# A hybrid decoder step: S5 constants on VectorE, power tables on GpSimd, q and k norms by head pairs, and the S5 state with chunks innermost

## The chip, the core and the metric

The kernel runs on one core of a Trainium2 chip (trn2). Five engines work at once: TensorE (PE in the profile; its weight loads are PEld), VectorE (DVE), ScalarE (ACT), GpSimd (POOL) and SyncE (SP, which here issues DMAs). Each takes its instructions strictly in the order in which the program issues them, and waits for semaphores of the others. The metric is the device time of one execution in microseconds (us).

## The reference

288 token columns (256 of a prompt, and 8 sequences of 4 sampled tokens) pass two layers of width 2048; everything is f32.

```python
# layer 0, first mixer
h = rmsnorm(x, w);  q, k, v, f, u = split(h @ w_in)          # 8 heads of 128; u is 1024 wide
q = rmsnorm(q, q_gain);  k = rmsnorm(k, k_gain)               # over the 128 of each head
logf = log_sigmoid(f + b_f)
att = softmax(q k^T * 128**-0.5 + cumsum(logf) differences, causal) v   # prompt; samples with a paged cache
# S5: 64 groups, 16 inputs and 64 complex states each, a diagonal recurrence over time
a = exp((lam_re + i*lam_im) * exp(log_dt));  z = (a - 1) / lam
s_t = a * s_(t-1) + (z*b) u_t;   y = Re(c s) + d*u;   ssm = gelu(y) * sigmoid(gelu(y) @ w_glu + b_glu)
x += concat(att, ssm) @ w_out
x += swiglu(rmsnorm(x))                                       # 5632 wide; layer 1: causal pooling mixer, then swiglu
```

The outputs also hold k, v, logf and the last S5 states.

## The kernel before, in words

**Weights and units.** Each f32 weight block of [128 x 512] arrives by a DMA of SP (`Ring.load`, L138), ScalarE rounds it to `wh` (L148), VectorE makes the rest `wl` = raw - wh (L149), and TensorE runs three products for each 128 x 128 piece (L186 to L188), whose right side has 288 columns. A *unit* is one such block: 12 matrix instructions. Three units are split ahead (`ring0.look`), in four buffers, so a VectorE that falls behind starves TensorE after three units.

**Ticks set the order.** After each unit `tick()` (L101) runs every pending evacuation, and then one step of each generator in `side`. A generator does some work, yields, and goes on one tick later; `W` holds how many ticks it lets pass. So all side work stands at a place in each engine's queue that this count fixes, whether or not its inputs are ready there. Units in order: 32 for u (ticks 1 to 32), one long one for f (33), 64 for q and k (34 to 97, a head in eight), 32 for v (98 to 129), 16 for the GLU, then w_out. When TensorE's side products are not ready, the units behind them wait too.

**First norm** (`gen_n0`, L372). With n0a = 3 the squares of x go into `acc` at ticks 4 to 11 (ScalarE squares, VectorE adds), and at tick 12 TensorE sums `accs` over partitions (L290). The rstd that comes of it is needed by the evacuations of u's first two blocks (`early`), and the fourth block can't begin before them.

**S5 constants** (`exp32`, `gen_s5_prep`, L417 to L537). Some 100 operations on [128 x 32] and [128 x 64] tiles make dt, |a|, sine and cosine, a's powers 1 to 4 and z: all on GpSimd, but for the reciprocal (L492), which VectorE runs at a fixed place. Then `steps`, `cross` and `times` make the tables a4x and a16x (a to the 4th and 16th), and VectorE forms bb = z*b.

**Power tables** (`powers`, L549). gt holds a^j * bb for j = 0 to 3 and p0 holds c * a^j for j = 0 to 4, real and imaginary part: 24 operations of up to [128 x 480] for gt and 24 of [128 x 512] for p0, all on VectorE, two of three followed by a yield. `gen_s5_g` turns gt by TensorE into gq (L648), and the products bb x p0 (L609) give the kernel of a block of four tokens (`kall`, `mt`).

**S5 over time** (`gen_s5_main`, L707). Time is cut into 64 chunks of four tokens. u goes through DRAM into `ut` (16 DMAs, half of them from GpSimd's queue). xt [73 chunks, 4, 2, 8] takes gq x ut (L750). Then `step` (L731, L735) joins four chunks at a time, three quarters on GpSimd and the last on VectorE; a chain of 15 steps on GpSimd runs over the blocks of four; `fill` (L779 to L785) carries it back into the chunks, one quarter on GpSimd and then three on VectorE. Their `tms` and `car` tiles have two buffers each that both engines share in program order. At last p0 x xt (L808) gives y. In each of these small products two of the array's four 64 x 64 quarters alternate.

**q and k norms** (`gen_qk`, L909), per head: square on ScalarE, split into `sh` and `sl` (VectorE, L917), four one-pass products with a matrix of ones (L922, L923), rsqrt on a tile that holds the sum on all 128 partitions, and two scalings.

Of the kernel before, what the change touches and what calls it, by code (L numbers as in the profile page):

```python
# [7 lines left out]
F32 = mybir.dt.float32  # L8
# [8 lines left out]
W = dict(n0a=3, n0b=0, n0c=0, n0d=2, rec=9, s5a=3, gq=0, xw=0, qk0=2, qk1=2, qk2=0, qk3=1, qk4=0, f=2, m=4, lag=2,  # L17
# [68 lines left out]
def hybrid_step(ctx, tc, I, O):  # L86
# [283 lines left out]
    n0 = Norm(x0, P_MIX0, pool0, "qs", bufs=2)  # L370

    def gen_n0():  # L372
# [8 lines left out]
        G.dma_start(bcd[:, 0], I["s5b"])  # L381
        G.dma_start(bcd[:, 1], I["s5c"])
# [27 lines left out]
    def gstt(out, a, c, b, op0, op1):  # L410

        t = small("stt", (128, 2, 2, 32), "tms", 2)[:, 0]
        t = t if len(out.shape) == 3 else t[:, 0]
        G.tensor_scalar(t, a, c, None, op0=op0)  # L414
        G.tensor_tensor(out, t, b, op1)

    def exp32(out, x):  # L417

        n, r, p = small("am"), small("den"), small("zt")
        e = pool0.tile([128, 32], I32, name="ei", tag="zu")  # L420
        G.tensor_scalar(n, x, 88.0, -87.0, op0=OP.min, op1=OP.max)
        G.tensor_scalar(r, n, 1.4426950408889634, MAGIC, op0=OP.mult, op1=OP.add)
        G.tensor_scalar(r, r, -MAGIC, None, op0=OP.add)
        gstt(p, r, -0.693359375, n, op0=OP.mult, op1=OP.add)
        G.tensor_scalar(e, r, 127.0, 8388608.0, op0=OP.add, op1=OP.mult)
        gstt(r, r, 2.12194440054690583e-4, p, op0=OP.mult, op1=OP.add)
        G.tensor_scalar(p, r, 1.0 / 5040.0, None, op0=OP.mult)
        for c in (1.0 / 720.0, 1.0 / 120.0, 1.0 / 24.0, 1.0 / 6.0, 0.5, 1.0):
            gstt(p, p, c, r, op0=OP.add, op1=OP.mult)
        gstt(out, p, 1.0, e.bitcast(F32), op0=OP.add, op1=OP.mult)  # L430

    def gen_s5_prep():
        lre, lim, ldt = (par[:, o:o + 32] for o in (P_LRE, P_LIM, P_LDT))
        dt, th, mag = small("dt"), small("th"), small("mag")
        exp32(dt, ldt)
        yield
        mul(mag, lre, dt, G)
        exp32(mag, mag)
        mul(th, lim, dt, G)
        yield  # L440
# [4 lines left out]
        for q in range(2):  # L445
            G.tensor_scalar(n[:, q], th, 1.0 / (2.0 * math.pi), 0.25 * q, op0=OP.mult, op1=OP.add)
        G.tensor_scalar(n, n, MAGIC, None, op0=OP.add)
        G.tensor_scalar(n, n, -MAGIC, None, op0=OP.add)
        thb = th[:, None, :].to_broadcast([128, 2, 32])
        gstt(r, n, -C1, thb, op0=OP.mult, op1=OP.add)  # L450
        gstt(r, n, -C2, r, op0=OP.mult, op1=OP.add)
        gstt(r, n, -C3, r, op0=OP.mult, op1=OP.add)
        G.tensor_scalar(r[:, 1], r[:, 1], math.pi / 2.0, None, op0=OP.add)
        yield
        mul(r2, r, r, G)
        fac = [math.factorial(k) for k in range(20)]
        G.tensor_scalar(sc, r2, 1.0 / fac[17], None, op0=OP.mult)
        for k in (15, 13, 11, 9, 7, 5, 3):
            gstt(sc, sc, (-1.0) ** (k // 2) / fac[k], r2, op0=OP.add, op1=OP.mult)
        gstt(sc, sc, 1.0, r, op0=OP.add, op1=OP.mult)  # L460
# [5 lines left out]
        mul(ap[:, 1, 0, :], mag, sc[:, 1], G)  # L466
        mul(ap[:, 1, 1, :], mag, sc[:, 0], G)

        def cross(dst, a):
            G.tensor_copy(dst[:, 0, 0, :], a[:, 0, :])  # L470
            G.tensor_scalar(dst[:, 0, 1, :], a[:, 1, :], -1.0, None, op0=OP.mult)
            G.tensor_copy(dst[:, 1, 0, :], a[:, 1, :])
            G.tensor_copy(dst[:, 1, 1, :], a[:, 0, :])

        cross(a1x, ap[:, 1])
        def times(out, a, bx):
            tm = small("tm", (128, 2, 2, 32), "tms", 2)
            mul(tm, a[:, None].to_broadcast([128, 2, 2, 32]), bx, G)
            add(out, tm[:, :, 0, :], tm[:, :, 1, :], G)

        for j in range(2, 5):
            times(ap[:, j], ap[:, j - 1], a1x)
        yield
        ar, ai = ap[:, 1, 0, :], ap[:, 1, 1, :]
        am, den, t, u = small("am"), small("den"), small("zt"), small("zu")
        zr, zi = small("zr"), small("zi")
        mul(den, lre, lre, G)
        mul(t, lim, lim, G)
        add(den, den, t, G)
        G.tensor_scalar(am, ar, -1.0, None, op0=OP.add)  # L490
        yield from ticks(W["rec"])
        V.reciprocal(den, den)  # L492
        yield
        mul(t, am, lre, G)
        mul(u, ai, lim, G)
        add(t, t, u, G)
        mul(zr, t, den, G)
        mul(t, ai, lre, G)
        mul(u, am, lim, G)
        G.tensor_tensor(t, t, u, OP.subtract)  # L500
        mul(zi, t, den, G)
# [11 lines left out]
        s5["a4"] = steps("a4x", ap[:, 4])  # L513
        a8 = small("a8", (128, 2, 32), "n")
        cross(a1x, ap[:, 4])
        times(a8, ap[:, 4], a1x)
        cross(a1x, a8)
        times(a8, a8, a1x)
        s5["a16"] = steps("a16x", a8)
        yield from ticks(W["s5a"])  # L520
# [21 lines left out]
        count = [0]  # L542

        def pace():
            count[0] += 1
            if count[0] % 3 != 1:
                yield

        def powers(dst, src, j0, pr, neg):  # L549

            nj = 4 if j0 else 3
# [1152 lines left out]
```

## Time and profile before

| | us |
|---|---|
| median of three runs | 2225.29 (2223.77 to 2228.7) |
| the profiled execution, its own time | 2224.44 |
| its span in the trace | 2222.6 |
| TensorE busy in the span | 2186.7 |
| mean granted TensorE clock | 0.995 |

Microseconds in the views count from the start of the span. An idle time in brackets behind a row names what released the instruction. "L149" is line 149 of the kernel before.

### The profile page before, as it was taken

What the parts mean: (1) busy time and instruction counts of PE and PEld (TensorE: products, weight loads), DVE (VectorE), ACT (ScalarE), POOL (GpSimd) and SP (SyncE); (2) the same over time, 40 slices, a digit from 0 to 9 for tenths busy, and PEclk for the clock granted to TensorE, in tenths of its full rate; (3) what the DMA queues carried; (4) which work ended last, traced back from release to release, by engine and by line L of the source; (5) the groups of instructions that cost most, each with busy time, mean ns of one, the idle gap of its engine ahead of it and who ended that gap; (6) DMA issues with size and microseconds to landing.
All of it is one profiled execution on the core that took longest, in us unless ns stands there. A gap on an engine that the chain in (4) does not pass through costs nothing.

```text
span 2222.6 us, 41005 instructions
## 1 busy us (share of the span) xinstructions
PE 2186.7 (98%) x17006; PEld 2146.2 (97%) x17006; DVE 1222.1 (55%) x1595; ACT 918.8 (41%) x1302; POOL 191.4 (9%) x297
## 2 busy tenths in 40 slices
PE   8998999999999999999999999999999999999999
PEld 7987988999999999999999998999999999999999
DVE  6987656655554545444554557555554455455443
ACT  5454545444333333333433355443333333333332
POOL 8365200100000000000000020000000000000000
PEclk9999999999999999999999999999999999999999
DMA  6637487555555555555555653555555555555554
GB/s 202 172 106 199 134 252 251 189 190 171 165 163 167 161 171 162 170 161 172 161 171 158 199 161 106 168 162 169 167 158 170 170 163 162 170 167 165 161 169 141
DMA packets 136715, 376.43 MB, mean 169 GB/s; under 512 B 22352, under 2 KB 26144, under 8 KB 136240
## 3 DMA queue, kind: packets, MB, share of 16 engines
q1 hardware_dynamic: 123008, 358.07, 53.9%
q10 hardware_dynamic: 11728, 11.27, 1.6%
q0 software_dynamic: 1792, 4.47, 0.7%
q8 instruction: 133, 2.18, 0.4%
q14 instruction: 54, 0.44, 0.1%
HBM read 364.34 MB, written 8.76 MB: 168 GB/s over the span
## 4 chain that ended last, share of the span: by engine, by line
PE 89%; POOL 3%; DVE 3%; DMA 2%; issue 1%; ACT 1%; SPq 0%; ACTq 0%; DVEq 0%; POOLq 0%
PE m L186 28%; PE m L188 28%; PE m L187 28%; DVE wl L149 1%; PE s L808 1%; POOL xt L735 1%; DMA pg<-in_vc_dram 1%; POOL stt L414 1%; DMA zs<-zscr 0%; POOL tms L731 0%; ACT wh L148 0%; DMA raw<-in_w_dram 0%; DMA raw<-in_wv_dram 0%; PE s L750 0%; DMA bl<-in_band_dram 0%
## 5 line engine op out<-in xcount | busy, mean ns | idle before, releaser
L149 DVE TENSOR_TENSOR wl<-raw,wh 128x1024 fp32r<-128x1024 f32 (+2 forms) x769 | 819.0, 1070 | 805.1 <-ACT wh L148 801.0
L148 ACT CAST wh<-raw 128x1024 fp32r<-128x1024 f32 (+2 forms) x769 | 692.4, 905 | 942.7 <-PE m L187 756.4
L188 PE MATMUL m<-xh,wl 128*128 128x288 f32 (+1 forms) x3312 | 979.6, 296 | 9.9 <-DVE wl L149 9.9
L186 PE MATMUL m<-xh,wh 128*128 128x288 f32 (+1 forms) x3312 | 987.4, 298 | 0.9 <-DVE x L221 0.9
L187 PE MATMUL m<-xl,wh 128*128 128x288 f32 (+1 forms) x3312 | 978.3, 295 | 0.0
L188 PEld LDWEIGHTS m<-xh,wl 128*128 128x128 f32 (+1 forms) x3312 | 622.5, 188 | 12.7 <-DVE wl L149 12.0
L186 PEld LDWEIGHTS m<-xh,wh 128*128 128x128 f32 (+1 forms) x3312 | 623.2, 188 | 8.6 <-issue 4.8
L187 PEld LDWEIGHTS m<-xl,wh 128*128 128x128 f32 (+1 forms) x3312 | 621.8, 188 | 0.9
L188 PE MATMUL m<-gh,wl 128*128 128x288 f32 x1408 | 415.7, 295 | 0.0
L187 PE MATMUL m<-gl,wh 128*128 128x288 f32 x1408 | 415.3, 295 | 0.0
L186 PE MATMUL m<-gh,wh 128*128 128x288 f32 x1408 | 414.7, 295 | 0.0
L186 PEld LDWEIGHTS m<-gh,wh 128*128 128x128 f32 x1408 | 264.5, 188 | 0.0
L188 PEld LDWEIGHTS m<-gh,wl 128*128 128x128 f32 x1408 | 264.4, 188 | 0.0
L187 PEld LDWEIGHTS m<-gl,wh 128*128 128x128 f32 x1408 | 264.2, 188 | 0.0
L215 ACT ACTIVATE s<-t 128x288 f32<-128x288 f32 x88 | 39.1, 444 | 169.9 <-DVE t L218 169.9
L1380 POOL DMA_DIRECT2D out_plo_dram<-es x1 | 0.6, 575 | 780.2 <-DVE wl L149 780.2
L218 DVE TENSOR_TENSOR t<-m,rstd 128x576 f32<-128x576 f32 x88 | 66.1, 751 | 0.0
L218 DVE TENSOR_TENSOR t<-s,t 128x288 f32<-128x288 f32 x88 | 40.3, 458 | 46.3 <-ACT s L215 46.3
L1336 DVE TENSOR_TENSOR gl<-t,gh 128x288 fp32r<-128x288 f32 x88 | 40.3, 458 | 44.0 <-ACT gh L1335 44.0
L221 DVE TENSOR_TENSOR x<-m,x 128x576 f32<-128x576 f32 x72 | 54.1, 751 | 8.8 <-PE m L188 8.7
L1335 ACT CAST gh<-t 128x288 fp32r<-128x288 f32 x88 | 38.1, 433 | 46.2 <-DVE t L218 46.2
L186 PE MATMUL m<-ssmh,wh 128*128 128x288 f32 x128 | 38.9, 304 | 0.8 <-ACT wh L148 0.8
(349 smaller groups left out, 1426.2 us busy)
## 6 DMA issues: line engine op xcount, KB each, us to landing
raw<-in_w_dram SPq DMA_DIRECT2D x472, 512.0 KB, 3.7
raw<-in_w_dram SPq DMA_DIRECT2D x64, 384.0 KB, 3.2
raw<-in_wqk_dram SPq DMA_DIRECT2D x64, 256.0 KB, 3.2
raw<-in_wout_dram SPq DMA_DIRECT2D x64, 256.0 KB, 3.2
raw<-in_wu_dram SPq DMA_DIRECT2D x32, 256.0 KB, 3.7
pg<-in_kc_dram SPq DMA_DIRECT2D x32, 256.0 KB, 3.4
raw<-in_wv_dram SPq DMA_DIRECT2D x32, 256.0 KB, 3.6
pg<-in_vc_dram SPq DMA_DIRECT2D x28, 256.0 KB, 4.1
```

The lines of the kernel that those rows point to most:

```text
L148: S.copy(h[:, :n], t[:, :n])
L149: self.share().tensor_tensor(l[:, :n], t[:, :n], h[:, :n], OP.subtract)
L186: T.matmul(o, h[:, w0:w0 + m], xh, start=st, stop=False)
L187: T.matmul(o, h[:, w0:w0 + m], xl, start=False, stop=False)
L188: T.matmul(o, l[:, w0:w0 + m], xh, start=False, stop=sp)
L215: S.activation(out, x, func, **kw)
L218: eng.tensor_tensor(out, a, b, OP.mult)
L221: eng.tensor_tensor(out, a, b, OP.add)
L414: G.tensor_scalar(t, a, c, None, op0=op0)
L735: eng.tensor_tensor(dst, dst, tv[:, :, :, c], OP.add)
L1335: S.copy(gs[c][0][:, i, :], t[:, 1, :])
L1336: V.tensor_sub(gs[c][1][:, i, :], t[:, 1, :], gs[c][0][:, i, :])
```

## The change

Everything lies in the first mixer, and the diff below is cut to its new side.

- The S5 constants run on VectorE: 72 operations, with a fused scalar-tensor-tensor in place of each pair on GpSimd, a few at each tick. Seven are issued ahead of the first unit, nine at tick 1, the last at tick 19.
- The first norm starts at tick 9 (n0a = 8), so TensorE's sum stands at tick 17 and `early` is over at tick 24.
- b and c are loaded by SP in the seventh unit, not by GpSimd.
- Of gt the imaginary half goes to GpSimd (12 operations), which then makes a4x and a16x; the real half stays on VectorE. All 24 operations of p0 go to GpSimd, issued at ticks 36 to 39, and bb x p0 stands at ticks 42, 43, 46 and 47.
- All 16 loads of `ut` are issued by ScalarE's queue.
- xt is [4, 16, 73] with the chunk innermost, so the right sides of L808 are contiguous; h0 goes through a `tms` tile.
- L609, L750 and L808 go round all four quarters of the array, into two PSUM banks.
- The q and k norms take two heads at a time: four f32 sums of 32 rows each into the four row groups of one bank, one rsqrt on [128 x 288], and per head two products of 32 rows that spread a row group's result over 128 partitions. The scaling then reads PSUM.

```diff
-W = dict(n0a=3, n0b=0, n0c=0, n0d=2, rec=9, s5a=3, gq=0, xw=0, qk0=2, qk1=2, qk2=0, qk3=1, qk4=0, f=2, m=4, lag=2,
+W = dict(n0a=8, n0b=0, n0c=0, n0d=2, gt=1, gq=0, xw=0, qk0=2, qk1=2, qk2=1, qk3=1, qk4=0, qk5=1, qk6=1, f=2, m=4, lag=2,
...
-        G.dma_start(bcd[:, 0], I["s5b"])
-        G.dma_start(bcd[:, 1], I["s5c"])
...
+    def vstt(out, a, c, b, op0, op1):
+        V.scalar_tensor_tensor(out, a, c, b, op0=op0, op1=op1)
...
-        G.tensor_scalar(n, x, 88.0, -87.0, op0=OP.min, op1=OP.max)
...
+        V.tensor_scalar(n, x, 88.0, -87.0, op0=OP.min, op1=OP.max)
+        V.tensor_scalar(r, n, 1.4426950408889634, MAGIC, op0=OP.mult, op1=OP.add)
+        V.tensor_scalar(r, r, -MAGIC, None, op0=OP.add)
+        yield
...
+        yield
+        for i, c in enumerate((1.0 / 720.0, 1.0 / 120.0, 1.0 / 24.0, 1.0 / 6.0, 0.5, 1.0)):
+            vstt(p, p, c, r, op0=OP.add, op1=OP.mult)
+            if i == 2:
+                yield
+        vstt(out, p, 1.0, e.bitcast(F32), op0=OP.add, op1=OP.mult)
+        yield
...
+        yield from exp32(dt, ldt)
+        mul(mag, lre, dt)
+        mul(th, lim, dt)
+        yield
+        yield from exp32(mag, mag)
...
-            times(ap[:, j], ap[:, j - 1], a1x)
-        yield
+            times(ap[:, j], ap[:, j - 1], a1x, V)
+            yield
...
+        mul(rden, lre, lre)
+        mul(t, lim, lim)
+        add(rden, rden, t)
+        V.reciprocal(rden, rden)
+        yield
...
+        apn = small("apn", (128, 5, 32))
+        G.tensor_scalar(apn, ap[:, :, 1, :], -1.0, None, op0=OP.mult)
...
+        def powers(eng, dst, part, src, j0, pr, neg=False):
...
+            if part == 0:
+                mul(dst, sr(src[:, 0]), re, eng)
+                yield
+                mul(t, sr(src[:, 1]), im, eng)
+                yield
+                eng.tensor_tensor(dst, dst, t, OP.subtract)
+            else:
+                mul(dst, sr(src[:, 0]), ni if neg else im, eng)
+                yield
+                mul(t, sr(src[:, 1]), re, eng)
+                yield
...
+        tens = [slice(q, min(q + 10, 32)) for q in range(0, 32, 10)]
+        for pr in tens:
+            for _ in powers(G, gtv(1, pr), 1, bb, 0, pr):
+                pass
+        s5["a4"] = steps("a4x", ap[:, 4])
+        a8 = small("a8", (128, 2, 32), "n")
+        cross(a1x, ap[:, 4], G)
+        times(a8, ap[:, 4], a1x, G)
+        cross(a1x, a8, G)
+        times(a8, a8, a1x, G)
+        s5["a16"] = steps("a16x", a8)
+        for pr in tens:
+            yield from powers(V, gtv(0, pr), 0, bb, 0, pr)
+        yield from ticks(W["gt"])
         side.append(gen_s5_g(gt))
         for q in range(0, 32, 8):
             pr = slice(q, q + 8)
+            for r in range(2):
+                for _ in powers(G, p0[:, pr, r, 16:].rearrange("p g (j c) -> p g j c", c=16), r, c, 1, pr, True):
+                    pass
+            yield
         yield from ticks(W["lag"])
         kall = pool0.tile([128, 16, 2, 64], F32, name="kall", tag="Y")
         mt = pool0.tile([128, 16, 2, 64], F32, name="mt", tag="M")
...
+        for e in range(2):
+            pss = [psum.tile([128, 512], F32, name=n, tag=n, bufs=b) for n, b in (("a", 1), ("s", 3))]
+            for d in range(8):
+                for r in range(2):
                     for h2 in range(2):
                         pair = 2 * (8 * e + d) + h2
+                        for g2 in range(2):
+                            T.matmul(pss[g2][64 * h2:64 * h2 + 16, d * 64:d * 64 + 64],
                                      bb[64 * g2:64 * g2 + 64, r, pair, :],
                                      p0[64 * g2:64 * g2 + 64, pair, r, 0:64], start=r == 0, stop=r == 1)
+                if d in (3, 7):
+                    yield
...
+    prep = gen_s5_prep()
+    for _ in range(2):
+        next(prep)
+    def gen_prep0():
+        for _ in range(2):
+            next(prep)
+        yield from prep
+    side.append(gen_prep0())
...
+        if j == 6:
+            SY.dma_start(bcd[:, 0], I["s5b"])
+            SY.dma_start(bcd[:, 1], I["s5c"])
...
-                for g2, e in enumerate((S, G)):
-                    e.dma_start(ut[p:p + 16, :, g2, :], uv[h2, 3 - j, :, :, g2, :])
+                for g2 in range(2):
+                    S.dma_start(ut[p:p + 16, :, g2, :], uv[h2, 3 - j, :, :, g2, :])
                 yield from ticks(W["uv"])
...
+        xt = poola.tile([128, 4, 16, 73], F32, name="xt", tag="big1")
...
+        G.dma_start(h0, I["h0"])
+        G.tensor_copy(xt.rearrange("p q x n -> p (q x) n")[:, :, 0:8], h0)
...
+            eng.tensor_tensor(tm.rearrange("p (o x n) -> p o x n", n=n, o=2),
+                              src[:, None].to_broadcast([128, 2, 16, n]), a, OP.mult)
+            tv = tm.rearrange("p (o c x) -> p o c x", o=2, c=2)
+            return [tv[:, :, c].rearrange("p o (g n) -> p o g n", n=n) for c in range(2)]
+        def step(eng, dst, src, a, n):
+            d = dst.rearrange("p (o g) n -> p o g n", o=2)
+            for t in parts(eng, src, a, n):
+                eng.tensor_tensor(d, d, t, OP.add)
+        def quarter(a, q, n):
+            return a[:, q][:, :, :, None].to_broadcast([128, 2, 16, n])
...
         yield from ticks(W["xw"])
         for q in range(4):
             gq = s5["g"][q]
+            for r in range(2):
+                pss = [psum.tile([128, 512], F32, name="s", tag="s", bufs=3) for _ in range(2)]
+                for d in range(4):
+                    for g2 in range(2):
+                        for h2 in range(2):
+                            k = slice(64 * h2, 64 * h2 + 64)
...
+            pss = [psum.tile([128, 512], F32, name="s", tag="s", bufs=3) for _ in range(2)]
+            for d in range(4):
+                for r in range(2):
+                    for h2 in range(2):
+                        pair = 2 * (4 * q + d) + h2
+                        for g2 in range(2):
+                            k = slice(64 * g2, 64 * g2 + 64)
...
+    qk = pool0.tile([128, NH, 2, NT], F32, name="qk")
+    qn, kn = qk[:, :, 0], qk[:, :, 1]
...
+    def gen_qk(h):
...
+            S.activation(sqs[i], qk[:, h + i], AF.Square)
...
+        ps = psum.tile([128, 512], F32, name="s", tag="s", bufs=3)
+        for g in range(4):
+            T.matmul(ps[32 * g:32 * g + 32, :NT], ones[:, :32], sqs[g // 2][:, g % 2], start=True, stop=True,
+                     skip_group_check=True)
+        yield from ticks(W["qk2"])
+        r = t2("r", shape=(128, 1, NT))
+        for i, _ in enumerate(rsqrt_steps([ps[:, :NT]], 128.0, r)):
+            yield from ticks(W[("qk3", "qk4")[i]])
+        yield from ticks(W["qk5"])
         for i in range(2):
...
+            pss = []
+            for j in range(2):
+                g = slice(64 * i + 32 * j, 64 * i + 32 * j + 32)
+                pss.append(psum.tile([128, 512], F32, name="s", tag="s", bufs=3))
+                T.matmul(pss[j][:, :NT], cst[g, C_ID + g.start:C_ID + g.start + 1].to_broadcast([32, 128]), r[g, 0],
+                         start=True, stop=True)
+            yield from ticks(W["qk6"])
+            for o, p, w in ((qn, pss[0], qgs), (kn, pss[1], par[:, P_KG:P_KG + 1])):
...
+            mul(qk[:, h], ps[:, :, :NT], rstd2)
+            if h % 2:
+                side.append(gen_qk(h - 1))
```

## Rows read from the trace of the kernel before

**Rows 1.** The page: busy times; summed matmuls overlap.
```profile
PE 2186.7 (98%) x17006; PEld 2146.2 (97%) x17006; DVE 1222.1 (55%) x1595; ACT 918.8 (41%) x1302; POOL 191.4 (9%) x297
```

**Rows 2.** Windows, 50 us each: engines' busy us (instructions), TensorE clock, DMA share, GB/s.
```profile
0.00:50.00 50.00, 39.27 (x249) 37.70 (x250) 29.47 (x55) 26.62 (x50) 40.30 (x108) 0.92 0.58 185
50.00:100.00 50.00, 49.29 (x367) 46.99 (x366) 47.45 (x95) 22.09 (x40) 22.14 (x36) 0.97 0.73 199
100.00:150.00 50.00, 48.53 (x621) 44.22 (x621) 44.35 (x69) 28.29 (x68) 32.75 (x32) 1.00 0.37 111
...
600.00:800.00 200.00, 200.00 (x1509) 200.00 (x1508) 100.81 (x108) 76.30 (x90) 0.00 (x0) 1.00 0.56 165
```

**Rows 3.** Waits of TensorE, us in total, times, longest.
```profile
PE m L188 <- DVE wl L149: 10.1, 10, 5.2
PE s L923 <- DVE sl L917: 4.3, 2, 4.1
```

**Rows 4.** Timeline, VectorE: start us, us, line, out<-in, count, idle before.
```profile
9.18 0.69 DVE L149 TENSOR_TENSOR wl<-raw,wh 128x512 fp32r<-128x512 f32 x1 [2.73 <-ACT wh L148]
...
45.81 0.35 DVE L492 RECIPROCAL den<-den 128x32 f32<-128x32 f32 x1 [9.30 <-POOL den L221]
...
57.90 0.68 DVE L535 COPY bcd<-tab 128x512 f32<-128x512 f32 x1
```

**Rows 5.** Timeline, TensorE, where it waited.
```profile
31.01 0.75 PE L290 MATMUL s<-accs,ones 128*128 128x288 f32 x2 [1.45 <-DVE accs L221]
...
46.76 0.61 PE L188 MATMUL m<-xh,wl 128*128 128x288 f32 x1 [5.21 <-DVE wl L149]
```

**Rows 6.** Windows where the clock was low.
```profile
45.00:50.00 5.00, 3.24 (x13) 3.24 (x14) 4.16 (x10) 0.00 (x0) 4.58 (x14) 0.59 0.48 150
...
200.00:210.00 10.00, 5.31 (x29) 4.68 (x31) 8.11 (x15) 3.35 (x6) 3.21 (x4) 0.83 0.78 218
```

**Rows 7.** Timeline, VectorE: short operations.
```profile
101.16 0.56 DVE L221 TENSOR_TENSOR fc<-fc,lf 8x8 f32<-8x8 f32 x3
...
115.23 0.25 DVE L1001 SCALAR_TENSOR_TENSOR cnr<-cnr,lfp,cst 128x32 f32<-128x32 f32 x1
```

**Rows 8.** Groups of GpSimd, 119 to 155 us, shapes apart.
```profile
L735 POOL TENSOR_TENSOR xt<-xt,tms 128x256 f32<-128x256 f32 x18 | 17.7, 985 | 1.4
L731 POOL TENSOR_TENSOR tms<-xt,a4x 128x512 f32<-128x512 f32 x9 | 14.2, 1577 | 12.4 <-ACT xs L756 11.9
```

**Rows 9.** Timeline, GpSimd.
```profile
50.57 0.21 POOL L507 COPY a4x<-apow 128x32 f32<-128x32 f32 x1
...
60.48 0.20 POOL L510 COPY a16x<-a 128x32 f32<-128x32 f32 x1
79.12 1.08 POOL L957 DMA_INDIRECT lfp<-in_lfc_dram,idx  x1 [18.43 <-DVE idx L953]
...
85.94 1.00 POOL L962 MEMSET qm<- 128x1056 f32 x1
```

**Rows 10.** VectorE's weight split, GpSimd idle (61 to 79 us), then busy (120 to 154).
```profile
L149 DVE TENSOR_TENSOR wl<-raw,wh 128x512 fp32r<-128x512 f32 x9 | 6.2, 686 | 0.9 <-ACT wh L148 0.9
...
L149 DVE TENSOR_TENSOR wl<-raw,wh 128x512 fp32r<-128x512 f32 x11 | 12.5, 1158 | 0.2 <-ACT wh L148 0.2
```

**Rows 11.** Timeline, TensorE: small matrix products, two instructions each.
```profile
102.39 0.38 PE L922 MATMUL s<-sh,ones 128*128 128x288 f32 x1
...
103.00 0.30 PE L186 MATMUL m<-xh,wh 128*128 128x288 f32 x1
...
130.09 1.08 PE L609 MATMUL a<-p,bcd 64*16 64x64 f32 x32
...
212.23 1.09 PE L851 MATMUL s<-ut,mt 64*64 64x72 f32 x28
...
245.99 4.79 PE L808 MATMUL s<-xt,p 64*64 64x72 f32 x64
```

**Rows 12.** Timeline, VectorE in the fill, waiting for GpSimd.
```profile
199.15 0.66 DVE L779 TENSOR_TENSOR tms<-xt,a4x 128x480 f32<-128x480 f32 x1 [2.53 <-POOL car L783]
```

More of the change, by code (lines that the diff above doesn't have):

```diff
@@ L369, in hybrid_step @@
     pt = pool0.tile([128, 18], I32, name="pt")
[L370 removed]
+    n0 = Norm(x0, P_MIX0, pool0, "qs")
     def gen_n0():
@@ L465, in gen_s5_prep @@
         G.memset(ap[:, 0, 1, :], 0.0)
[L466 to L479, printed above, removed]
@@ new lines, in gen_s5_prep, with times @@
+        cross(a1x, ap[:, 1], V)
+        yield
+        def times(out, a, bx, eng):
+            tm = small("tm" if eng is G else "tmv", (128, 2, 2, 32), *(("tms", 2) if eng is G else ()))
+            mul(tm, a[:, None].to_broadcast([128, 2, 2, 32]), bx, eng)
+            add(out, tm[:, :, 0, :], tm[:, :, 1, :], eng)
+        for j in range(2, 5):
+            times(ap[:, j], ap[:, j - 1], a1x, V)
+            yield
+        ar, ai = ap[:, 1, 0, :], ap[:, 1, 1, :]
+        am, t, u = small("am"), small("zt"), small("zu")
@@ L511, in steps @@
             return dst.rearrange("p q o c g -> p q o (c g)")
[L513 to L520, printed above, removed]
         b = bcd[:, 0].rearrange("p r (g c) -> p r g c", c=16)
@@ L594, in gen_s5_prep @@
             pr = slice(q, q + 8)
-            yield from powers([p0[:, pr, r, 16:].rearrange("p g (j c) -> p g j c", c=16) for r in range(2)],
-                              c, 1, pr, True)
+            for r in range(2):
+                for _ in powers(G, p0[:, pr, r, 16:].rearrange("p g (j c) -> p g j c", c=16), r, c, 1, pr, True):
+                    pass
+            yield
         yield from ticks(W["lag"])
@@ L720, in gen_s5_main @@
         xs = pool0.tile([128, 8, 4, 2, 8], F32, name="xs")
[L721 to L724 removed]
+        xb = xt[:, :, :, 9:].rearrange("p q x (b j) -> p q x b j", j=4)
+        h0 = pool0.tile([128, 64, 8], F32, name="h0", tag="tms", bufs=2)
+        G.dma_start(h0, I["h0"])
+        G.tensor_copy(xt.rearrange("p q x n -> p (q x) n")[:, :, 0:8], h0)
@@ new lines, in step, with chain @@
+        def step(eng, dst, src, a, n):
[4 more added lines that the diff above has]
+            return a[:, q][:, :, :, None].to_broadcast([128, 2, 16, n])
+        def chain(dst, src):
+            tm = pool0.tile([128, 512], F32, name="tms", tag="tms", bufs=2)[:, :128]
+            G.tensor_tensor(tm.rearrange("p (q o x) -> p q o x", q=4, o=2),
+                            src[:, :, None, :].to_broadcast([128, 4, 2, 16]), a16, OP.mult)
+            tv = tm.rearrange("p (q o c g) -> p q o c g", q=4, o=2, c=2)
+            d = dst.rearrange("p q (o g) -> p q o g", o=2)
@@ L792, in gen_s5_main @@
         for q in range(4):
-            step(G, xs[:, :, q], xt[:, 0:8, q].rearrange("p n r g -> p n (r g)"), quarter(a4, q, 8), [8])
+            step(G, xs[:, :, q].rearrange("p n r g -> p (r g) n"), xt[:, q, :, 0:8], quarter(a4, q, 8), 8)
         G.dma_start(O["s5s"], xs)
@@ new lines, in gen_qk @@
+        sqs = []
+        for i in range(2):
+            sqs.append(t2("sq"))
+            S.activation(sqs[i], qk[:, h + i], AF.Square)
+        yield from ticks(W["qk1"])
+        ps = psum.tile([128, 512], F32, name="s", tag="s", bufs=3)
[4 more added lines that the diff above has]
+        r = t2("r", shape=(128, 1, NT))
```

242 lines of the change are left out of this document (74 added, 168 removed).

## The prediction

> **What bounds the kernel now.** I read the busy times first, then windows, then the waits of TensorE, and at last the timelines around the longest of them. TensorE is busy for 2186.7 of 2222.6 us [rows 1], so some 36 us without work can be won at most, besides its own small products and what a low clock costs. From 600 to 800 us 1509 matrix instructions take 200 us, 0.1325 us each, so a unit of twelve takes 1.59 [rows 2]: the later stages are full. The missing time lies in the first mixer, where TensorE idles 10.7 of the first 50 us and VectorE is busy for 47 and 44 of the next two 50 [rows 2]. The waits name VectorE: 10.1 us for `wl`, 5.2 of them at once, and 4.3 us for `sl` [rows 3]. The 5.2 us end at 46.8 [rows 5], and the reason stands on VectorE: it waited 9.30 us for GpSimd's `den` [rows 4]. TensorE's clock then fell to its lower level, 0.59 in the five us from 45, and again to 0.83 in the ten from 200, after the wait for `sl` [rows 6]. The last costs 10 x 0.17 = 1.7 us, the first some 3.
>
> **Part by part.** All sums are against the profiled execution's 2224.4 us, 0.9 below the median of 2225.3.
>
> *Constants on VectorE, first norm later.* VectorE gets 72 short operations. Three dependent ones of 8 columns take 0.56 us in all, 0.20 from start to start, and one of 32 columns lasts 0.25 [rows 7]. Many have 64 or 128 columns, so I take 0.24; bounds 0.16 and 0.30. Of the 72, 16 fall into idle time before 9.2 us [rows 4]. The other 51 up to tick 17 cost 51 x 0.24 = 12.2 us. `accs` was ready at 31.0 at tick 12 [rows 5]; at tick 17 it follows five more `wl` of 0.69 [rows 10] as well: 31.0 + 3.4 + 12.2, less 0.9 of small idle pieces used, is 45.7. TensorE came there at 31.0 - 1.45 = 29.6 [rows 5]; now five units later (8.0), and the first eight units, paced by VectorE, end 2.3 later (4.5 of constants, less three adds of 0.73 moved out): 39.8. So it waits 45.7 - 39.8 = 5.9 us, about what it waited before (1.45 + 5.21), again with a fall of the clock behind it. It resumes at 46.8 with unit 18, where before it had unit 19: 1.6 us lost. VectorE then has per tick one `wl`, the last constants, the forming of bb and the two early evacuations. By the same prices it frees the PSUM buffer for unit 25 at 62.1, where TensorE would come at 60.9: another 1.2. **Front: +2.8**, from -5 (0.16 each, wait gone) to +6 (0.30). The reciprocal's stall goes, and the late `accs` takes its place. The 1 MB of b and c on SP costs nothing, since the DMA share is 0.58 in the first 50 us [rows 2] and `wl` runs late anyway; without that cover it is its transfer time, 1 MB at 185 GB/s or 5 us.
>
> *Tables on GpSimd.* bb is ready at about 58, as before (57.9 + 0.68, [rows 4]). From there GpSimd has a queue. Nine operations of 480 columns and three of 96 for gt: a product of 512 columns takes 1.58 while VectorE works beside it, a sum of 256 takes 0.985 [rows 8]; 9 x 1.42 + 3 x 0.4 = 14. Then a4x and a16x, which took 50.6 to 60.7 before [rows 9]: 18 instead of 20 operations, 9. That is 81. The gathers for `lfp` need an index that VectorE makes after the f unit, at about 82.5, and with the memset behind them take 79.1 to 86.9, 7.8 us [rows 9]: 90.5. Then p0: 24 operations. Bounds: 1.3, the rate of the 256-column sum with a third off for its short rows, and 1.97, twice that sum. I take 1.5, near the 512-column product: 36, so p0 ends at **126.5**.
>
> "GPSIMD Engine Reference" of the Trainium skill (Engine selection) says that GpSimd is about twice as slow as VectorE for two inputs; by it p0 is an estimated 24 x 2 x 0.69 = 33 us, 3 less than my sum. The same page (Specifications) has the two engines contend when VectorE reads two SBUF inputs, and this speaks against the change; the trace agrees, since `wl` takes 0.686 with GpSimd idle and 1.158 with it busy [rows 10].
>
> That contention holds VectorE at about 2.1 us a tick (1.16 for `wl`, 0.9 for the real half of gt) from 58 to 72, 0.5 over a unit; three units of lead hide most, and I charge TensorE 2. Then it has unit 25 at 62.1, eight units (12.7), 2, the f unit (6.4), fourteen units (22.3), transposes and the products themselves (4.8): it would finish unit 47 at 110.3. But bb x p0 stands at ticks 42, 43, 46 and 47 in TensorE's own queue, and each takes a quarter of p0. Three or four waits follow, 126.5 - 110.3 = **16 us**, with all weight products queued behind them. Before, unit 46 ended just before 102.4 [rows 11], so unit 47 at about 106: the change is 20 behind here, with everything above included.
>
> *What comes back.* (a) L609 is already done there; before it still had eight pieces of 1.02 us [rows 11]: -8.2. (b) L808: 64 instructions in 4.72 us (0.074 each), while L851, contiguous and over two quarters of the array, needs 1.02 for 28 (0.036) [rows 11]. 256 x 0.037 = -9.5; if four quarters halve it again, -14.2; I take -11. (c) L750 runs at L851's rate already; four quarters may give 0 to -5, taken -3. (d) The waits behind unit 47 that the trace of before has: some 4 for `wl`, 4.3 for `sl`, 3 of smaller ones [rows 3], and 1.7 of clock [rows 6]: -13. `sl` is gone, and VectorE has 22 us less to do between 60 and 125; what is late next is GpSimd. (e) Norms: eight one-pass products per two heads were 8 x 0.133. Now four f32 sums over column tiles and four f32 spreads; an f32 product is two instructions and took 0.38 us from start to start [rows 5]. Side by side 1.7, one after another 3.6; so +0.6 a pair, at worst +2.5: **+2.5** in all. (f) GpSimd starts `step` at about 135 instead of 119, as some 9 us of memset, DMAs and h0 stand between; 31 for three quarters and 27 for the chain, a little under before, bring the fill to VectorE at about 201, where it was at 199.2 after waiting 2.5 [rows 12]. VectorE reaches that place (tick 80) at about the same time, since TensorE does the 33 units from 126.5 in 52.5 plus 20 of small products. So the wait there is small, but the last quarter of `step` on VectorE shares two `tms` buffers with GpSimd and waits: +2.5, and +2 for a fall of the clock after the p0 waits.
>
> 20 - 8.2 - 11 - 3 - 13 + 2.5 + 2.5 + 2 = **-8.2**: 2216.2 for such an execution, 2217 against the median. The layers behind have the same instructions and stay.
>
> **Rivals.** *GpSimd becomes the bound (slower).* Place: p0 and all that GpSimd has behind it. If its operations cost what the 256-column sum costs for each column, 1.97 for 512, p0 ends 11 us later, TensorE waits 27 and VectorE's fill comes 10 late, on the same path: -8 + 11 + 5 of further wait and clock = 2232. It decides from a mean of about 1.85 us. For it: in-place sums are dear [rows 8], and a third of the new work is such. Against: products are not. *The waits stay short.* Constants at 0.16 and p0 at 1.3 end p0 near 115: -8 - 11 = 2206. For it: the short operations could overlap where they don't depend on each other. Against: nearly all do. *The products gain nothing:* if L808 is slow through its accumulation and not its stride, the 11 stay: 2227, no change. Against: L609 also accumulates and runs at 0.032 [rows 11].
>
> **Chances.** Forecast 0.43 (its own range 2210 to 2224), GpSimd bound 0.22, short waits 0.20, no gain in the products 0.15. A measurement tells 0.2%, 4.5 us: faster means under 2220.8, slower over 2229.7. Faster: three quarters of the forecast, all of the short waits, 0.54. Slower: most of GpSimd's case and a little of the others, 0.22. Same: 0.24. The range reaches from 2203 to 2234.
>
> **What would show it.** Right: L290 waits 4 to 7 us near 40 to 46; L492's wait on GpSimd is gone; TensorE has waits on GpSimd's p0 at L609's successor of together 10 to 20 us before 130; p0's operations average 1.4 to 1.7; L808's successor takes 5 to 10 us in all; no row for `sl`. Wrong: if TensorE waits for p0 under 5 us, the gain is larger, and the front or GpSimd's prices were mis-sized; if VectorE's fill or the last `step` keeps TensorE over 8 us, GpSimd is the bound and the change loses.

## The result, and the profile after

The changed kernel takes 2252.6 us (median of four runs) against 2225.7 for the one before: 1.011 times as long, 95% interval 1.0093 to 1.0128. Forecast were 2217 us, 2203 to 2234: it lies outside this range, and the change loses where it was to win. The profiled execution takes 2254.9 us, its span 2253.1, at a mean clock of 0.983.

I go through the views in the order of the prediction. TensorE's busy time on the page has grown by 5 us only [rows 1]; this sum shows neither the waits nor that the same instructions ran at a lower clock:

```profile
PE 2191.7 (97%) x17038; PEld 2142.5 (95%) x17038; DVE 1215.4 (54%) x1602; ACT 900.4 (40%) x1280; POOL 193.6 (9%) x222
```

The windows of the first mixer, which answer to [rows 2]; behind them two more of the kernel before:

```profile
0.00:50.00 50.00, 39.66 (x233) 37.24 (x234) 37.63 (x118) 25.79 (x47) 1.34 (x7) 0.94 0.64 202
50.00:100.00 50.00, 47.53 (x347) 44.90 (x345) 44.00 (x74) 20.09 (x37) 38.71 (x43) 0.96 0.59 159
100.00:150.00 50.00, 39.96 (x649) 35.89 (x648) 34.38 (x41) 20.82 (x50) 46.15 (x38) 0.93 0.37 92
150.00:200.00 50.00, 38.17 (x343) 33.48 (x344) 27.29 (x35) 18.01 (x40) 38.72 (x56) 0.83 0.50 135
200.00:250.00 50.00, 41.45 (x339) 34.91 (x338) 41.26 (x78) 18.26 (x38) 21.68 (x30) 0.92 0.51 159
...
600.00:800.00 200.00, 200.00 (x1508) 200.00 (x1508) 102.26 (x110) 77.26 (x93) 0.00 (x0) 1.00 0.55 164
```

```profile
150.00:200.00 50.00, 47.10 (x466) 42.11 (x462) 37.84 (x56) 22.64 (x40) 37.48 (x57) 1.00 0.70 169
200.00:250.00 50.00, 44.55 (x439) 40.63 (x439) 40.50 (x72) 28.62 (x49) 12.76 (x17) 0.97 0.68 205
```

From 600 to 800 us nothing has changed. From 100 to 250 TensorE works 40, 38 and 41 of each 50 us, and the clock, 1.00, 1.00 and 0.97 before, is 0.93, 0.83 and 0.92. From 100 to 200 VectorE is less busy than before, GpSimd more (46 instead of 33 from 100 to 150); from 200 to 250 VectorE is as busy as it was. What TensorE waited for in the first 420 us, in total, times, longest [rows 3]:

```profile
PE s L959 <- DVE r L322: 12.1, 2, 8.4
PE a L615 <- POOL p L573: 8.4, 2, 4.5
PE s L879 <- ACT ym L884: 6.9, 1, 6.9
PE s L290 <- DVE accs L221: 5.2, 1, 5.2
PE s L1090 <- DVE nl L1070: 2.7, 1, 2.7
PE m L187 <- DVE zt L1276: 2.6, 1, 2.6
```

Of `wl` (9 us up to 420) 2 are left, and `sl` has gone, as forecast. Two waits of the new list were forecast: `accs`, and GpSimd's `p`. Two were not: `r`, the result of the new norm, and `ym`, the evacuation of the direct product. In or right behind both the clock stands low (windows as above; 0.66 over 15 us is 10.2 us at half clock):

```profile
185.00:200.00 15.00, 8.51 (x85) 7.22 (x86) 2.60 (x4) 5.41 (x10) 12.80 (x29) 0.66 0.51 153
240.00:255.00 15.00, 8.22 (x44) 6.15 (x45) 12.57 (x25) 4.47 (x11) 9.69 (x13) 0.66 0.56 167
```

From here on I use a ledger of TensorE, worked out from the start times of its instructions: weight products (`main`), all other products (`small`), waits (gaps over 0.55 us between two starts), and `clock`, half of the low-clock time outside the waits. It is one profiled execution of each kernel, so a us or two of a difference means little. It goes from the first unit to the start of unit 161, behind the first mixer. us:

| kernel | total | main | small | waits | clock |
|---|---|---|---|---|---|
| before | 393.8 | 275.2 | 86.6 | 25.7 | 6.4 |
| after | 419.2 | 277.2 | 66.0 | 57.7 | 18.3 |

The products gave back 20.6 us. The waits took 32.0 and the clock 11.9. By stretch (units counted from 0: 0 to 33, 33 to 49, 49 to 101, 101 to 113, 113 to 161) the change costs +4.6, +17.5, +14.1, -20.7 and +9.9. The -20.7 is mainly a move: the output product, 18.8 us at units 102 to 105 before, now takes 4.7 us at units 97 to 100, in the stretch ahead of it. Some 5 us more come later, most of them from low clock between 1340 and 1410 us in layers whose instructions are the same. They go with the execution rather than with the change: between 1310 and 1420 us the traces of all the kernels here hold from 3.4 to 20.4 us of low clock, 20.4 in the changed kernel and also in e5 below, and 3.4 in e8, which is the changed kernel with less work.

### The profile page after: what moved, and what is told of

Its sections match the earlier page's. It is cut to its first block, busy times and chain, and to the rows that moved or that the text cites. A ratio compares the mean times of both kernels' runs of the same rounds, so it can differ in the third digit from the quotient of the medians.

```text
span 2253.1 us, 40977 instructions
## 1 busy us (share of the span) xinstructions
PE 2191.7 (97%) x17038; PEld 2142.5 (95%) x17038; DVE 1215.4 (54%) x1602; ACT 900.4 (40%) x1280; POOL 193.6 (9%) x222
## 4 chain that ended last, share of the span: by engine, by line
PE 80%; DMA 1%; DVE 1%; ACT 1%; issue 0%; SPq 0%; ACTq 0%; DVEq 0%
PE m L188 26%; PE m L187 26%; PE m L186 26%; DVE wl L149 1%; ACT wh L148 0%; DMA raw<-in_w_dram 0%; DMA out_v_dram<-vn 0%; DMA bl<-in_band_dram 0%; DVE zl L1525 0%; DMA raw<-in_wout_dram 0%; PE m L1536 0%; PE a L1114 0%; PE m L1513 0%; PE m L1515 0%; PE m L1514 0%
```

## The experiments

"Before" and "after" stand for the two kernels; ratios are to before, as it ran beside each version, with their 95% interval. The edits are shown abridged, with comments and `...` for what is left out. The theories as they stood at first: *A*, the waits arise where pieces of side work meet in an engine's queue; *B2*, GpSimd's lateness is the root; *C*, the new norm is.

**e1: the products alone.** Before, with the new layout of `xt` and the new orders of the three products.

> The kernel before with the new S5 state layout and the new order of the three products (bb x p0, xt, output) and nothing else; constants, tables and norms as before. Theory A (the products gain what the changed kernel's trace shows, 14 us at the output product, 4 at xt and 4 at bb x p0, and the loss lies in waits that the other parts bring): 2225.7 - 22 = 2204, with some of it turned into waits 2202 to 2212. Theory B (the new layout itself makes the steps dearer on GpSimd and VectorE, or the products' time was cover for something else): 2220 to 2232.

Measured 2236.7, 1.0049 (1.0032 to 1.0067): slower than before by 10, and above what either theory expected (2204 and 2220 to 2232). Small products fell from 86.6 to 63.3, and waits rose from 25.7 to 48.8, the clock's loss from 6.4 to 12.6. The waits are VectorE's:

```profile
PE m L188 <- DVE wl L149: 14.5, 12, 5.2
PE s L933 <- DVE sl L927: 12.0, 4, 4.8
```

Theory A falls in this form: the products' gain doesn't reach the end even without the other parts. What took its place, *A2*, is stated with e5.

**e2: the old norms in the changed kernel.**
```diff
-    side.append(gen_qk(h - 1))          # one tile of sums for two heads
+    side.append(gen_qk(h, qk[:, h]))    # per head: sh, sl, four products
```

> The changed kernel with the q and k norms of before (per head, sh and sl, one-pass products). Theory A (the 12.1 us that TensorE waits for r are VectorE's backlog and would turn up at another of its results): 2241 to 2250. Theory C (the new norm is the cause, since its second product puts TensorE behind VectorE's r twice per pair of heads): the 12.1 us and the two falls of the clock behind them (3.4 and 5.1 us) go, 2252.6 - 20 = 2232 or less.

Measured 2249.9, 1.0106 (1.0088 to 1.0124). The 12.1 us for `r` are gone, and 14.7 for `wl` and 4.6 for `sl` stand in their place: C falls. The norm was only where VectorE's lateness showed.

**e3: p0 on VectorE in the changed kernel.**
```diff
-    for _ in powers(G, p0[...], r, c, 1, pr, True): pass
+    yield from powers(V, p0[...], r, c, 1, pr, True)     # and bb x p0 in the old order
```

> The changed kernel with p0's 24 operations on VectorE as before, and bb x p0 in the old order, since the new one would hold PSUM buffers against the later xt products. Theory B2 (GpSimd, late by p0, is the root of all later waits): 2228 or less. Theory A: the two waits for p0 (8.9 us) and the clock behind them (3.4) go, the old order costs 4 more, VectorE is fuller, the page loads and the norms still wait: 2238 to 2248.

Measured 2250.2, 1.0106 (1.0086 to 1.0127), no better than after. Units 33 to 49 take 31.0 us instead of 47.7, so the waits for p0 with all that hung on them were worth 16.7. All of it is lost again behind, 8.3 of it from unit 113 to 161, where the GLU now waits for the S5 output (its load lands 10.3 us after 329.2):

```profile
PE m L186 <- ACT zt L1272: 8.8, 1, 8.8
PE s L957 <- DVE r L322: 8.3, 2, 5.3
...
PE a L1051 <- POOL xt L813: 5.4, 1, 5.4
```

With the tables paced by ticks on VectorE, the S5 chain starts later (the output product at unit 107 instead of 97) and misses its own date, the GLU at unit 129. The 2228 of B2 did not come, and 2250 lies above A's range too. Since the edit also moved the chain, it can't tell what GpSimd's lateness alone would have cost; it shows that taking p0 from GpSimd gains nothing here.

**e4: the first key pages spread out in the changed kernel.**
```diff
-        ahead()
+        for _ in range(3):
+            tiles.append(load_page(*pages.pop(0)))
+            yield from ticks(2)
```

> The changed kernel with the first three key pages (six DMAs, 6.5 us in a row on SP's queue) loaded one page each second tick. Theory A (these six keep SP from the next weight block, ScalarE waits for that block with the evacuation of the direct product behind it, and TensorE for the evacuation): the wait of 6.9 us near 184 is under 1.5 and the low clock of 10.2 us behind it goes: 2252.6 - 7 - 5 = 2241, 2238 to 2244. Theories B2 and C: the next late engine takes its place, 2249 to 2253.

Measured 2248.7, 1.0104 (1.0084 to 1.0124). The wait for `ym` fell from 6.9 to 1.7, which settles the cause of this wait. In the changed kernel SP issues six page loads in a row, and ScalarE holds the evacuation back behind the cast of a block that SP hasn't fetched (timelines of SP, then of ScalarE):

```profile
179.68 6.46 SPq L1004 DMA_DIRECT2D pg<-in_kc_dram  x6
186.25 7.57 SPq L138 DMA_DIRECT2D raw<-in_wqk_dram  x6
...
190.34 0.62 ACT L148 CAST wh<-raw 128x512 fp32r<-128x512 f32 x1 [8.65 <-DMA raw<-in_wqk_dram]
190.87 1.17 ACT L884 COPY ym<-s 64x504 f32<-64x504 f32 x2
```

The same six loads stood in the kernel before, without harm: there the direct product came 19 units later (87 instead of 68), when the loads were long done. But the time is at most 4 us less, not 12, and the two intervals (1.0093 to 1.0128 for after) don't tell even that from nothing; in the ledger a new wait of 3.2 for `qm` came up. This place is worth less than its wait.

**e5: the order of the output product alone, in the kernel before.**
```diff
-            for g2 in range(2):
-                for d in range(4): for r in range(2): for h2 in range(2): T.matmul(ps[g2] ...)
+            for d in range(4): for r in range(2): for h2 in range(2):
+                for g2 in range(2): T.matmul(pss[g2] ...)      # old layout of xt
```

> The kernel before with one edit: the output product alternates between the two halves of the state rows (four quarters of the array in turn), in the old state layout. Theory A2 (VectorE's queue, and not the products, bounds TensorE from unit 49 to unit 101, so that time taken from products there turns into waits, and each longer wait lowers the clock; only at the output product, units 103 to 106, where VectorE is busy 20 of 40 us, is a gain kept): the product takes about 9 instead of 18.8 us and the gain stays, 2215 to 2220. Theory E (no shorter product pays, since VectorE is late everywhere): 2223 to 2229.

Measured 2220.4, 0.9962 (0.9949 to 0.9976): the fastest of all versions. Small products fell by 8.4 us and nothing else moved (waits 23.9, clock 6.1).

**e6: the orders of bb x p0 and xt alone, in the kernel before.**

> The kernel before with the new orders of bb x p0 and xt alone, in the old state layout: 8.1 and 10.4 us of products become about 4 and 6. Theory A2: no gain, the 8 us turn into waits for VectorE with falls of the clock behind them, 2226 to 2235. Rival (the order pays where it stands, and the loss of the run with the products alone came from the layout): 2217 to 2221.

Measured 2236.9, 1.0036 (1.0023 to 1.005). Products 9.5 less, waits 9.8 more, clock 5.7 more. The first place where it falls behind is unit 53. VectorE's timeline from 117, first of the kernel before, then of e6:

```profile
117.86 0.69 DVE L218 TENSOR_TENSOR p<-bcd,apow 128x512 f32<-128x512 f32 x1
118.47 0.69 DVE L218 TENSOR_TENSOR a<-bcd,apow 128x512 f32<-128x512 f32 x1
119.07 0.69 DVE L149 TENSOR_TENSOR wl<-raw,wh 128x512 fp32r<-128x512 f32 x1
119.67 0.68 DVE L572 TENSOR_TENSOR p<-p,a 128x512 f32<-128x512 f32 x1
120.27 1.25 DVE L917 TENSOR_TENSOR sl<-sq,sh 128x576 fp32r<-128x576 f32 x1
```

```profile
117.95 1.23 DVE L218 TENSOR_TENSOR p<-bcd,apow 128x512 f32<-128x512 f32 x1
119.10 1.24 DVE L218 TENSOR_TENSOR a<-bcd,apow 128x512 f32<-128x512 f32 x1
120.25 1.74 DVE L149 TENSOR_TENSOR wl<-raw,wh 128x512 fp32r<-128x512 f32 x1
121.92 0.67 DVE L572 TENSOR_TENSOR p<-p,a 128x512 f32<-128x512 f32 x1
122.51 0.75 DVE L919 TENSOR_TENSOR sl<-sq,sh 128x576 fp32r<-128x576 f32 x1
```

Three operations in front of `sl` take 0.69 in one and 1.23 to 1.74 in the other, and `sl` starts 2.2 us later. Not every operation is slowed (`p<-p,a` and, in e6, `sl` are not), and in the kernel before the same slowing comes right behind, from `sl` on. What differs beside them is GpSimd's first `step`, of before and of e6:

```profile
119.07 1.84 POOL L731 TENSOR_TENSOR tms<-xt,a4x 128x512 f32<-128x512 f32 x1 [11.93 <-ACT xs L756]
```

```profile
116.19 1.29 POOL L731 TENSOR_TENSOR tms<-xt,a4x 128x512 f32<-128x512 f32 x1 [9.16 <-ACT xs L757]
```

The new order of xt hands over two tiles at once, so GpSimd starts 2.9 us earlier, and VectorE meets it with p0's operations still in its queue. TensorE then waits 3.3 us at 120 and 2.3 at 127 (1.5 there before), and the clock falls twice for 3.4. This became theory *A3*.

**e7: the new layout alone, in the kernel before.**

> The kernel before with the new state layout and all products in the old order: the output product reads contiguous columns, VectorE's and GpSimd's steps write strided ones (5 us more on VectorE, 4 on GpSimd). Theory A2: 9 us are won at the output product, the 5 of VectorE cost some 5 to 10 with the clock, 2222 to 2229. Rival (the layout is what lost 10 us in the run with the products alone): 2231 to 2238.

Measured 2227.0, 1.0002 (0.999 to 1.0014), as A2 had it. Small products fell by 12.0; VectorE's and GpSimd's operations on strided columns became dearer (VectorE's add of 240 columns 0.68 instead of 0.50 us on average), waits rose by 4.5 and the clock's loss by 6.5.

**e8: the changed kernel without VectorE's fills** (27 operations, ticks kept).
```diff
-        for q in (1, 0, 2, 3):
-            yield from fill(G if q == 1 else V, q)
+        yield from fill(G, 1)
+        yield from ticks(9)
```

> The changed kernel without the three fills that run on VectorE (left out: the carried states of three quarters; all ticks stay). Theory A (the 8.4 us wait for r near 240 is VectorE's queue, filled by 27 fill operations that GpSimd's lateness and the norms' later place bring together): the wait is under 2 and the 10.2 us of low clock behind it go: 2252 - 8 - 5 = 2239, 2235 to 2243. Theories B2 and C (GpSimd's or the norms' own place): 2247 to 2253.

Measured 2240.5, 1.0062 (1.0041 to 1.0082), 12 less than after (11 by the ratios). Of the 12.1 us for `r` 3.7 are left, and units 49 to 101 take 136.0 instead of 146.8. So the 8.4 us near 240 are VectorE's queue, and not GpSimd: that engine had ended its own share of the fill at 214.3 and idled until 240.6. In the changed kernel the queue reads, with the fill's operations in between:

```profile
241.06 0.45 DVE L312 TENSOR_SCALAR v<-s 128x288 f32<-128x288 f32 x1
...
242.07 0.97 DVE L749 TENSOR_TENSOR tms<-car,a4x 128x480 f32<-128x480 f32 x1
...
245.95 0.78 DVE L322 SCALAR_TENSOR_TENSOR r<-q,y 128x288 f32<-128x288 f32 x1
```

TensorE stood at the second product of that norm from 238.0.

**e9: e6 with its products issued twice.**
```diff
-                for r in range(2):          # bb x p0
+                for r in (0, 1, 0, 1):      # and each xt product twice
```

> The kernel before with the new orders of bb x p0 and xt, each of these products issued twice into the same place (the second writes the same values again), so that TensorE has 10 us more to do than in the run with the new orders alone (2236.9). Theory A2 (the stretch is bound by VectorE, and what TensorE does there replaces waiting and keeps the clock up): the waits from unit 49 to 101 fall from 20 to about 10 us, the clock loses 3 instead of 8, 2236.9 + 10 - 10 - 5 = 2232, 2226 to 2237. Rival (the products are on the path and the new orders cost something of their own): 2244 to 2249.

Measured 2243.1, 1.0062 (1.0048 to 1.0075). Neither side was right: the doubled products cost 6 of the 10 us meant (the trace has 8 us more of products), and the waits from unit 49 to 101 stayed (19.8 after 19.6). TensorE's extra time is not taken out of the waits one for one. It was this that spoke against plain slack, and for something that the new orders do to VectorE itself.

**e10: e6 without VectorE's share of the S5 state.**

> The kernel before with the new orders of bb x p0 and xt, and without VectorE's share of the S5 state (left out: the nine operations of the last quarter's step and 27 of the three fills; all ticks stay), some 23 us of VectorE. Theory A2: the waits for sl and wl between 162 and 178 and between 207 and 238, some 12 us, go with the clock's falls behind them, 5 us: 2236.9 - 17 = 2220, 2214 to 2227. Rival (the waits are due to the products' order or to GpSimd): 2232 to 2238.

Measured 2226.0, 0.9989 (0.9979 to 0.9999): 11 less than e6, at the upper edge of what A2 expected; units 49 to 101 take 133.1 instead of 142.3. VectorE's load does set these waits; the one at 121 (3.4), where nothing was taken away, stayed.

**e11: e5 with a later reciprocal.**
```diff
-rec=9
+rec=14
```

> The kernel before with the new order of the output product (2220.4) and the reciprocal of the S5 constants five ticks later on VectorE. Theory A2: where VectorE reaches the reciprocal, GpSimd's den (45.8) is ready, so the 5.2 us stall and the 3.4 us of the low clock behind it go, and what follows keeps its time: 2220.4 - 8 = 2212, 2208 to 2216. Rival (the tables come later into VectorE's full stretch, and the time won at 46 is given back as waits between units 49 and 101): 2218 to 2226.

Measured 2246.8, 1.0082 (1.0069 to 1.0096): both sides wrong. Up to unit 33 it wins 5.8 us on e5, as expected, with no fall of the clock. Up to unit 113 all of this is gone, as the rival had it. Then 27.7 us are lost from unit 113 to 161. As in e3, five ticks at the head of the S5 chain make its end miss the GLU, which is 7.8 of them; further waits (4.2 for `att`) and falls of the clock follow, whose causes no run takes apart:

```profile
PE m L186 <- ACT zt L1241: 7.8, 1, 7.8
```

**e12 and e13: without GpSimd's steps, for before and for e6.**
```diff
-                step(V if q == 3 else G, ...)
+                if q == 3:
+                    step(V, ...)
```

> Control: the kernel before without GpSimd's share of the steps (left out: the 27 operations that join four chunks in three quarters of the state; GpSimd's other work stays). Theory A3 (VectorE's operations take 1.23 instead of 0.69 us while GpSimd works beside them, so GpSimd's hours set VectorE's): VectorE wins some 6 us between 119 and 155, of which TensorE's waits show 1.5 to 4: 2222 to 2227. Rival (no contention that matters): 2226 to 2229.

> The kernel before with the new orders of bb x p0 and xt, and without GpSimd's share of the steps (left out as in the control). Theory A3 (the new order of xt hands two quarters over at once, GpSimd starts at 116.2 instead of 119.1 and slows VectorE while p0's operations still stand in its queue): the waits near 120 and 127 (3.3 and 2.3) and the low clock behind them (3.4 us lost) go, 2236.9 - 9 = 2228 or less, within 4 us of the control. Rival (the order itself costs: ScalarE's paired evacuations, PSUM buffers): it stays 8 us over the control, 2231 or more.

Measured 2227.4 (1.0, 0.9992 to 1.0009) and 2226.7 (0.9994, 0.9983 to 1.0006). Without the steps the two come out alike: the new orders cost nothing, where with the steps they cost 8 to 9 us. The control itself gained nothing, where A3 expected 2222 to 2227: in the kernel before, the contention costs no time that shows. In e13 VectorE's operations of the same place take 0.69 again, and the waits at 120 and 127 are down to 1.0 and 1.1:

```profile
120.41 0.69 DVE L218 TENSOR_TENSOR p<-bcd,apow 128x512 f32<-128x512 f32 x1
121.02 0.70 DVE L218 TENSOR_TENSOR a<-bcd,apow 128x512 f32<-128x512 f32 x1
121.62 0.69 DVE L149 TENSOR_TENSOR wl<-raw,wh 128x512 fp32r<-128x512 f32 x1
122.22 0.68 DVE L572 TENSOR_TENSOR p<-p,a 128x512 f32<-128x512 f32 x1
122.82 0.76 DVE L920 TENSOR_TENSOR sl<-sq,sh 128x576 fp32r<-128x576 f32 x1
```

That is A3, at this place. That the two engines contend is also what the Trainium skill says ("GPSIMD Engine Reference", Specifications: VectorE with two SBUF inputs contends with GpSimd); the runs agree, 0.69 against 1.23 for one operation. Yet the 7.6 us that e13's products save on e12's don't show in its time, so more than this contention holds TensorE there; the next run has a part of it.

**e14: the orders of the output product and of bb x p0, xt as before.**

> The kernel before with the new orders of the output product and of bb x p0, xt as before. Theory A3: bb x p0 releases nothing on GpSimd before the mask adds, so its 4 us are kept or turn into waits, but the 10 us loss doesn't appear: 2216 to 2222. Rival (any time taken from products between units 49 and 101 is lost with the clock): 2223 to 2232.

Measured 2223.5, 0.9981 (0.9971 to 0.9991), just inside the rival's range. The 10 us loss doesn't appear, so the larger part of it belongs to xt's order; but the 4 us of bb x p0 aren't kept either, and it lies 3 to 4 behind e5, with intervals that just overlap. The trace shows where. Waits of about 1.5 us for `sl` at unit 69, 2.6 for `zt` at 129 and 2 for a value page at 136 stand in e14, e6, e9 and e13 alike, all with the new order of bb x p0, while before, e5 and e12 have at most 1.1 at any of the three. The one for `zt`, in e14, then in e5:

```profile
PE m L187 <- DVE zt L1243: 2.6, 1, 2.6
```

```profile
PE m L187 <- DVE zt L1243: 0.8, 1, 0.8
```

The new order yields 8 times and not 12, so the direct product behind it stands four units earlier (83 instead of 87). Whether the order or this move makes the waits, no run tells apart.

## Why the prediction was wrong

**The front was right.** `accs` lets TensorE go on at 46.4 (predicted 46.8) after 5.2 us (5.9). +4.6 us up to unit 33 against +2.8.

**GpSimd's tables were right.** p0 ends at 124.6 (126.5), its 24 operations take 35.6 us (36, mean 1.48):

```profile
L218 POOL TENSOR_TENSOR tmp<-bcd,apow 128x512 f32<-128x512 f32 x8 | 10.6, 1321 | 0.0
L567 POOL TENSOR_TENSOR p<-p,tmp 128x512 f32<-128x512 f32 x4 | 7.1, 1784 | 0.3
L573 POOL TENSOR_TENSOR p<-p,tmp 128x512 f32<-128x512 f32 x4 | 7.1, 1767 | 0.3
L218 POOL TENSOR_TENSOR p<-bcd,apn 128x512 f32<-128x512 f32 x4 | 5.5, 1364 | 0.0
L218 POOL TENSOR_TENSOR p<-bcd,apow 128x512 f32<-128x512 f32 x4 | 5.3, 1314 | 0.0
```

By the Trainium skill's factor ("GPSIMD Engine Reference", Engine selection) it had been an estimated 33; the trace is nearer to the rows. TensorE is 22.2 us behind at unit 49; 20 were predicted. The end of p0 sets this, whatever TensorE does until then, so the agreement is p0's price and not the split, which was off: two waits, 8.4 us in all, and not three or four of 16; the rest are the front, 3.4 of clock and some 4 of bb x p0 itself, which stands there now. So the rival in which GpSimd is the bound, though it had the sign, had another place: p0's mean was far from its 1.85.

**The products came out as forecast in sum, partly by luck.** From one start to the next the output product takes 4.7 us instead of 18.8 (-14.1, forecast -11), xt 6.3 instead of 10.4 (-4.1, -3), and bb x p0 about 1.0 a piece, four pieces instead of eight. Taken together small products fell by 20.6; the prediction's terms, norms included, made 19.7. It counted 8.2 for bb x p0, of which 4 were saved, and 3 too few for the output product. The rival in which they gain nothing (2227, no change) named the wrong reason, accumulation: e7 takes the stride alone away and wins 11 us at this product. The time then failed to appear for another reason.

**The step that failed is (d), "the waits behind unit 47 that the trace of before has: -13", and what was said to come late next.** I took 13 us off because the operations that TensorE had waited for were gone, and let GpSimd alone be late. With (f), waits and low clock behind unit 49 were to fall by 8.5 us. Against that, the changed kernel's waits from unit 49 to 101 rise from 11.1 to 26.0 us and the clock's loss from 1.7 to 6.7; with the tail below they rise by 31 up to unit 161. These 39 us are more than the whole miss of 36. What TensorE waited for were ends of VectorE's queue, and any result in it can be that end. e2 shows it by exchange: `r` goes, `wl` and `sl` come. The wait for `sl` that (d) struck out was of this kind: in the kernel before, VectorE's fill, waiting for GpSimd, stood in front of `sl` (TensorE waited until 206.2), and the fill stayed:

```profile
201.58 0.41 DVE L783 TENSOR_TENSOR car<-tms 128x240 f32<-128x240 f32 x1 [1.77 <-POOL tms L779]
...
205.36 0.75 DVE L917 TENSOR_TENSOR sl<-sq,sh 128x576 fp32r<-128x576 f32 x1
```

Nor did the 22 us less on VectorE between 60 and 125 come about: it is busy for 54.3 instead of 62.2 us, 8 less, because beside GpSimd's new work each split takes longer. Before, then after:

```profile
L149 DVE TENSOR_TENSOR wl<-raw,wh 128x512 fp32r<-128x512 f32 x29 | 20.3, 700 | 2.3 <-ACT wh L148 1.8 <-issue 0.6
```

```profile
L149 DVE TENSOR_TENSOR wl<-raw,wh 128x512 fp32r<-128x512 f32 x25 | 24.9, 1004 | 7.3 <-ACT wh L148 7.3
```

Three places make most of the new waits: VectorE's fills in front of a norm (e8: 11 to 12 us with the clock), the page loads of SP in front of the direct product (e4: its wait falls by 5, the time by 4 at most), and the norm at 149.3 (4.0 us, no run of its own). The prediction's sign of being wrong, that VectorE's fill keeps TensorE over 8 us, came, but GpSimd was not the bound there (e8): (f) had put this fill at about 201, and it starts at 217.5, 3 us after GpSimd's share was done. Why the products' gain did not pay: in the kernel before, VectorE's pace depends on when GpSimd works, and a quicker xt makes the two meet earlier (e6 against e13), and bb x p0's order brings waits of its own (e14). In the changed kernel, where p0 is on GpSimd, no run takes this apart; that the gain is lost there in the same way is argued from e1, not shown. At units 102 to 105 of the kernel before VectorE has time, and there the gain is kept (e5).

**The clock was charged 2 us, 1.7 were taken off, and it took 11.9 more.** In the changed kernel it stood low in ten stretches of 3.4 to 10.2 us from 40 to 402 us, each of them in or right behind waits of TensorE of together 2.6 to 8.8 us. The trace of before already had two such pairs [rows 6]; a new wait should have been charged with a fall, 1.7 to 5.1 us. Not every wait brings one: those of 1.3 and 2.4 us before 12.4 bring none in this trace, and in e4's the same ones do.

**The tail was charged nothing.** Units 113 to 161 lose 9.9 us, 5.8 of waits and 5.1 of clock. The samples' page products stand four units later than before. The S5 output is not late, though: its load lands at 327.1, but on VectorE operations of scores and attention stand in front of `zt`, from 337.2 to 341.7, and TensorE waits 2.6 us for it. The same wait is in e14, which has nothing of the change but two product orders. No run changes this stretch of the changed kernel alone, so the cause of the 9.9 is read from the trace and not shown. e3 and e11 show how sharp that end is, 8 and 28 us for a chain that starts some ticks later.

## What to carry to other kernels

Before time taken off one engine is counted as won, look whether the stretch is held by another engine's queue: there a gain may be lost, and can even cost, since it can start a third engine earlier and make the second one slower (e6). A wait stands for the whole queue in front of the result that is waited for, so it doesn't go with that result. Count a long wait with a fall of the clock. Take the gain where the other engines have time: the one reordered loop of e5 gave 7 us, all the parts together lost 27.

## What the runs showed that I had not expected

- VectorE's two-input operation of 512 columns takes 0.69 us beside an idle GpSimd and mostly 1.2 to 1.75 beside a busy one, so with GpSimd's work starting 2.9 us earlier TensorE's waits there went from 1.5 to 5.6 us, with two falls of the clock.
- Alternating between the four quarters of the array and reading contiguous columns brought an instruction of the output product from 0.073 to 0.018 us from start to start; the order alone (e5) to 0.043, the layout alone (e7) to 0.031.
- Doubling the products in a stretch full of waits did not shorten the waits (19.8 after 19.6 us).
